# The end of a top-k decode put in another order: low parts of U made by VectorE, three transposes into one PSUM bank, one rounding by ScalarE, four stores on another queue

## The chip, the cores and the metric

One core of a Trainium2 chip runs the whole kernel. The metric is the device time of one execution in microseconds (us). Engines are named as in the profile: PE is TensorE, PEld its weight loads, DVE VectorE, ACT ScalarE, POOL GpSimd, SP SyncE, which only issues DMAs.

## What is computed

One encoder layer over 512 tokens: a projection, a spatial gating branch and an attention branch, and then a product-key expert layer (PEER). Only the last one touches the change:

```python
def block(xb):                                  # 128 tokens
    q = (xb @ w_query).reshape(PEER_TOKEN_BLOCK, PEER_HEADS, 2, D_KEY // 2)
    s = jnp.einsum('thpc,pkc->thpk', q, sub_keys)
    s1, i1 = lax.top_k(s[:, :, 0], PEER_TOPK)
    s2, i2 = lax.top_k(s[:, :, 1], PEER_TOPK)
    cand = (s1[..., :, None] + s2[..., None, :]).reshape(..., PEER_TOPK * PEER_TOPK)
    sc, ci = lax.top_k(cand, PEER_TOPK)
    e = (take_along_axis(i1, ci // PEER_TOPK) * N_KEYS + take_along_axis(i2, ci % PEER_TOPK))
    g = jax.nn.softmax(sc, axis=-1)
    act = jax.nn.gelu(jnp.einsum('td,thkd->thk', xb, expert_u[e]))
    return jnp.einsum('thk,thkd->td', g * act, expert_v[e])
```

There are 8 heads, 16 picks for each, 128 x 128 experts, width 1024.

## The kernel before

Three of the four token blocks (384 tokens) take the expert layer densely. For each of 128 slabs of 128 experts (here **unit** n, `prog["u"]`) TensorE multiplies the slab of U with the normed tokens. To keep float32 accuracy, U is cut into a high part and a low part: ScalarE casts `uraw` to `uhi` (`part`, L171), and `uraw - uhi` gives `ulo` (`part_lo`, L182). `product` (L202) then issues 24 matmuls of 128x384: 16 read `uhi`, the last 8 read `ulo`. `uraw`, `uhi`, `ulo` and the PSUM tiles `pu` have two buffers each, so `uhi` of unit n+2 may be written when the 16 of unit n are done, and the load of `uraw` n+2 when the low part of n is made. `flush` lets ScalarE read a finished unit through Gelu (`act`, L789) and so frees its bank. `ahead(n, limit)` issues the next n of these matmuls: it fills TensorE wherever other work is waited for, and 31 units (744 matmuls) are to be done by the end of the stretch described here.

The low part has two ways. While `prog["pool"]` is true, GpSimd makes it in two halves, the second half issued inside the product before. Once it is false, `los()` issues it whole on VectorE at the place where `los()` is called.

All engines run their instructions in program order. That order is written out by hand:

1. The loop over 16 query columns: query product, `scores`, two rounds of top 16 on VectorE (`top16`), candidates (`cand`, L648), `pick_head`. Every third head it appends a `decode`: a generator that turns positions into key indices and yields between its pieces. The pieces are: the position arithmetic on VectorE (L670 to L688), copies of `rw` and `cl` by ScalarE (L697, L698), comparisons and products on VectorE (L702 to L707), sums on VectorE (L711 to L717, which write `route`).
2. The decode's end: the pieces of heads 3 to 5 and then of heads 6 and 7, the softmax of the gates (`softmax`, L723 to L730) and stretches of `ahead` between.
3. `turn(0)`: `route` of the first block is transposed (L845), ScalarE writes the two index rows `idxT` and the gate `gT`, and VectorE rounds the gate (`gw`, L857) and takes the rest.
4. The pick loop, 48 slices of 8 tokens: VectorE makes one-hot rows `ohb` (L880) and weighted ones `oha` (L884), ScalarE the last two rows of `oha` (L895), TensorE multiplies them (L931, 16 small matmuls), ScalarE takes the result to `wst` (L911), which is stored to `wd`. Between the slices stand `ahead` calls that spread the rest of the 744 matmuls evenly, and `los()`.
5. After it the last four stores to `wd`, units 31 to 35 and then, to the end of the kernel, one loop in which unit products alternate with products with V (L1090).

Of the kernel before, what the change touches and what calls it, by code (L numbers as in the profile page):

```python
# [27 lines left out]
NK = 128  # L28
# [10 lines left out]
AHEAD = 31  # L39
GSCALE = 32768.0  # L40
# [6 lines left out]
def peer_block(ctx: ExitStack, tc: tile.TileContext, A, out):  # L47
    nc = tc.nc
    V, S, G, T, Q = nc.vector, nc.scalar, nc.gpsimd, nc.tensor, nc.sync
# [7 lines left out]
    pr = pr_ctx.enter_context(tc.tile_pool(name="pr", bufs=1, space=PSUM))  # L57
# [6 lines left out]
    wd = dram.tile([NWC, 128, NK, WTOK], F32, name="wd")  # L64
# [70 lines left out]
    ident = keep.tile([128, 128], F32, name="ident")  # L135
# [3 lines left out]
    iota_b = keep.tile([128, NK], BF16, name="iota_b")  # L139
# [37 lines left out]
    def part_lo(i, eng=G):  # L177

        if i in halves:
            hi, lo = parts[i]  # L180
            k = slice(4 * halves[i], 4 * halves[i] + 4 if eng is G else KT)
            eng.tensor_tensor(lo[:, k, :], raws[i][:, k, :], hi[:, k, :].bitcast(F32), op=ALU.subtract)  # L182
            halves[i] += k.stop // 4 - halves[i]
            if halves[i] == 2:
                del raws[i], halves[i]

    def los():
        for i in list(halves):
            part_lo(i, V)
# [116 lines left out]
    ps = []  # L306
# [30 lines left out]
    ps = []  # L337
# [5 lines left out]
    turning = heads_T("q", rot)  # L343
# [19 lines left out]
    ps = []  # L363
# [5 lines left out]
    turning = heads_T("k", rot)  # L369
# [14 lines left out]
    ps = []  # L384
# [10 lines left out]
    for b in range(NB):  # L395
        t = va[:, b, :]
# [76 lines left out]
    ps = []  # L473
# [91 lines left out]
    for b in range(NB):  # L565
        t = hs[b] = tk.tile([128, 1024], F32, name="xs", bufs=4)
# [45 lines left out]
    rt = rt_ctx.enter_context(tc.tile_pool(name="rt", bufs=1))  # L612
# [8 lines left out]
    def top16(lists):  # L621

        for m, ix, s in lists:
            V.max(m[:, 0:8], s)
        for m, ix, s in lists:
            V.max_index(ix[:, 0:8], m[:, 0:8], s)
        for m, ix, s in lists:
            V.match_replace(s, m[:, 0:8], s, NEG)
        for m, ix, s in lists:
            V.max(m[:, 8:16], s)  # L630
        for m, ix, s in lists:
            V.max_index(ix[:, 8:16], m[:, 8:16], s)
# [87 lines left out]
    def softmax(pool, top, g):  # L720

        PK = list(top.shape)
        V.tensor_tensor(g, top, top[:, :, :, 0:1].to_broadcast(PK), op=ALU.subtract)  # L723
        yield
        S.activation(g, g, AF.Exp)
        yield
        sm = pool.tile([128, 2, PK[1], PK[2]], F32, name="gsum")
        V.tensor_reduce(sm[:, 0], g, axis=AX.X, op=ALU.add)
        V.reciprocal(sm[:, 1], sm[:, 0])
        V.tensor_tensor(g, g, sm[:, 1, :, :, None].to_broadcast(PK), op=ALU.mult)  # L730
        yield
# [3 lines left out]
    route = [rt.tile([128, DB, H, TOPK], F32, name=f"route{i}") for i in range(3)]  # L735
# [30 lines left out]
    steps = []  # L766

    def step():
        while steps:
            if next(steps[0], True) is None:  # L770
                return
            steps.pop(0)

    def pick_head(h):
        cand = cands.pop(h)
        top16([(top[:, h, b, :], ci[:, h, b, :], cand[:, b, :]) for b in range(DB)])
        h0 = 0
        for n in HG:
            if h == h0 + n - 1:
                steps.append(decode(rt, iota_v, dense[1][:, h0:h0 + n], ci[:, h0:h0 + n], [r[:, h0:h0 + n] for r in by_head]))  # L780
            h0 += n
# [3 lines left out]
    def flush():  # L785
        if prog["gelu"] is not None:
            e, o = prog["gelu"]
            acts[e] = ring.tile([128, DT], F32, name="act")
            S.activation(acts[e], o[:, :DT], AF.Gelu_apprx_tanh)  # L789
            prog["gelu"] = None  # L790

    def ahead(n, limit):

        while n > 0:
            if prog["gen"] is None:
                if prog["u"] >= min(limit, NK):
                    return
                i = prog["u"] + NQ
                load(i + 2)
                part(i + 1)  # L800
                prog["gen"] = product(i, DT)
            o = next(prog["gen"])
            n -= 1
            if o is not None:
                flush()
                prog["gelu"] = (prog["u"], o)
                prog["gen"] = None
                prog["u"] += 1

    for c in range(NQ + 1):  # L810
# [4 lines left out]
        if c >= 1:  # L815
# [4 lines left out]
                cands[(c - 1) // 2] = candidates(rt, dense, (c - 1) // 2)  # L820
            elif c > 1:
                pick_head((c - 1) // 2 - 1)
    while steps:
        ahead(24, AHEAD)
        flush()
        step()
    pick_head(H - 1)
    gating = softmax(rt, top, by_head[2])
    next(gating)
    step()  # L830
    for _ in range(4):
        ahead(36, AHEAD)
        flush()
        next(gating, None)
        step()
    assert not steps or next(steps[0], True)
    tsc = {}

    def turn(b):

        rows = []
        for nm, t, dt, scale in (("i2T", route[1], BF16, 1.0), ("i1T", route[0], BF16, 1.0),
                                 ("gT", route[2], F32, GSCALE)):
            ps = pr.tile([128, 512], F32, name="po" if nm == "i2T" else "tr")
            T.transpose(ps[:, :128], t[:, b].rearrange("p h k -> p (h k)"), ident)  # L845
            if nm == "i2T":

                idx = rt.tile([128, 16, 2, 8, 2], BF16, name="idxT", bufs=2)
            r = idx[:, :, len(rows), :, :] if dt is BF16 else rt.tile([128, 16, 8, 2], F32, name=nm)
            S.activation(r, ps[:, :128].rearrange("p (g t) -> p g t", t=8)[:, :, :, None].to_broadcast([128, 16, 8, 2]),  # L850
                         AF.Copy, scale=scale)
            rows.append(r)
        gT = rows[2]
        yield

        gw = rt.tile([128, 16, 8, 2, 2], F16, name="gw", bufs=2)
        V.tensor_copy(gw[:, :, :, 0], gT)  # L857
        V.tensor_tensor(gw[:, :, :, 1], gT, gw[:, :, :, 0], op=ALU.subtract)

        gs = rt.tile([128, 16, 2], F32, name="gs", bufs=2)  # L860
        V.tensor_copy(gs[:, :, 0], gw[:, :, 7, 0, 0])
        V.tensor_tensor(gs[:, :, 1], gT[:, :, 7, 0], gs[:, :, 0], op=ALU.subtract)
        tsc[b] = (idx, gw, gs)
        yield

    drain(turn(0))
    prog["pool"] = False


    half = [128, 16, NK // 2, 2]  # L870

    def hots(t8):


        b, g = divmod(t8, 16)
        idx, gw, gs = tsc[b]
        pairs = lambda t: t.rearrange("p s t two -> p (s t) two")[:, :, None, :].to_broadcast(half)
        c = rt.tile([128, 16, NK], BF16, name="ohb", bufs=3)
        a = rt.tile([128, 16, NK], F16, name="oha", tag="oh", bufs=3)
        V.tensor_tensor(c.rearrange("p s (k two) -> p s k two", two=2),  # L880
                        iota_b.rearrange("p (k two) -> p k two", two=2)[:, None, :, :].to_broadcast(half),
                        pairs(idx[:, g]), op=ALU.is_equal)
        wide = [128, 7, 2, NK // 2, 2]
        V.tensor_tensor(a[:, 0:14].rearrange("p (t s) (k two) -> p t s k two", s=2, two=2),  # L884
                        c[:, 8:15, None].rearrange("p t o (k two) -> p t o k two", two=2).to_broadcast(wide),
                        gw[:, g, 0:7, :, None, :].to_broadcast(wide), op=ALU.mult)
        rest.append((a, c, gs, g))
        return a, c
# [9 lines left out]
    N8 = DT // 8  # L898
    per = WTOK // 8
    wst = None  # L900
    hot = [hots(0), hots(1)]
    gated()
    ahead(24, AHEAD)
    los()
# [8 lines left out]

    full = None

    def store(j):

        n = NK // per
        S.dma_start(wd[full[0], :, j * n:(j + 1) * n, :], full[1][:, j * n:(j + 1) * n, :])

    for t8 in range(N8):
        a, c = hot.pop(0)
# [3 lines left out]
        for q in range(2):  # L926
            pw = pr.tile([128, 4, NK], F32, name="acc", bufs=4)
            for j in range(4):
                for s in range(2):
                    t = 4 * q + j  # L930
# [7 lines left out]
        if t8 % 16 == 8 and t8 // 16 + 1 < DB:  # L938
            turning = turn(t8 // 16 + 1)
# [7 lines left out]
        if t8 % per == per - 1:  # L947
            full = (t8 // per, wst)
        if full is not None and t8 + 1 < N8:
            store((t8 + 1) % per)  # L950
    for j in range(per):
        store(j)
    ahead(10 ** 6, AHEAD)
    rt_ctx.close()
    pr_ctx.close()
# [204 lines left out]
    for e in range(NK):  # L1160
# [18 lines left out]
        n = min(int(quota), 128 - dotted)  # L1179
# [18 lines left out]
        if e == NK - 8:  # L1198
            assert issued == 128
            fg, *rest = [upool.tile([128, 1024], F32, name="fin", tag=t) for t in ("uraw", "uhi", "ulo") for _ in range(2)]  # L1200
            last = ex.tile([128, 2, 1024], F32, name="fin", tag="uv", bufs=UVB)
# [97 lines left out]
```

## Time and profile before

| | |
|---|---|
| median of 3 runs | 1474.46 us (1473.89 to 1474.46) |
| profiled execution | 1474.9 us, span 1473.1 us |
| PE busy | 1449.5 us (98%) |
| PEld busy | 1291.3 us (88%) |
| DVE busy | 1152.5 us (78%) |
| ACT busy | 658.0 us (45%) |
| POOL busy | 278.3 us (19%) |

The span runs from the first to the last instruction; the time of the execution has 1.8 us around it. Busy time of PE is modelled: its matmuls overlap, so the start of one and the start of the next say more than a length. In the rows below, what stands in brackets is the idle time of the engine before the row and who ended it.

### The profile page before, as it was taken

Reading aid. Unit: us, or ns where it says so; the run is one execution under the profiler, and the core shown is the slowest. Engines: PE = TensorE matmul, PEld = TensorE weight load, DVE = VectorE, ACT = ScalarE, POOL = GpSimd, SP = SyncE. Lnnn points to the kernel's source line nnn. Section 1 sums busy time; section 2 is a strip of 40 time slices with the busy share of each in tenths; the row PEclk is TensorE's granted clock in tenths of the full one; section 3 lists DMA queues with packets and bytes.
Section 4 is the critical chain, followed back from the end, with each engine's and each line's share of the span. In section 5 each row is a group of like instructions: output and inputs, shape, how many; then the busy total and the mean of one; then the engine's idle time right before and its main releaser. Section 6 shows DMA issues by size and latency. Waiting matters only on the chain.

```text
span 1473.1 us, 21706 instructions
## 1 busy us (share of the span) xinstructions
PE 1449.5 (98%) x7945; PEld 1291.3 (88%) x7945; DVE 1152.5 (78%) x2434; ACT 658.0 (45%) x1186; POOL 278.3 (19%) x222
## 2 busy tenths in 40 slices
PE   8999999999999999999999999999999999999997
PEld 6878988888999999999999999999999999988785
DVE  5745554999899949779888878888888888877865
ACT  4456743344578754433333333333333333333334
POOL 0140002445400000013131222222222222221000
PEclk9999999999999999999999999999999999999999
DMA  6331032232367776579999998999999999988764
GB/s 232 113 103 36 23 130 104 74 97 92 115 248 267 275 276 215 165 264 368 351 332 336 330 341 318 335 332 345 331 336 339 327 326 338 321 299 302 232 215 152
DMA packets 129067, 358.54 MB, mean 243 GB/s; under 512 B 9152, under 2 KB 59840, under 8 KB 112576
## 3 DMA queue, kind: packets, MB, share of 16 engines
q1 hardware_dynamic: 103328, 197.49, 40.5%
q0 software_dynamic: 18432, 134.23, 23.8%
q10 hardware_dynamic: 7200, 25.44, 4.3%
q8 instruction: 62, 1.02, 0.3%
q14 instruction: 45, 0.37, 0.1%
HBM read 327.10 MB, written 30.02 MB: 242 GB/s over the span
## 4 chain that ended last, share of the span: by engine, by line
PE 82%; DVE 11%; ACT 3%; issue 2%; DMA 1%; POOL 1%; ACTq 0%; SPq 0%; POOLq 0%; DVEq 0%
PE acc L1090 34%; PE pu L202 32%; PE acc L253 8%; DVE ohb L880 3%; DVE ulo L182 2%; DVE oha L884 2%; PE pu L253 1%; PE tr L440 1%; PE acc L453 1%; PE po L453 1%; DMA vraw<-in_uv_dram 1%; POOL ulo L182 1%; ACT uhi L171 1%; DMA uraw<-in_uT_dram 1%; PE pu L419 0%
## 5 line engine op out<-in xcount | busy, mean ns | idle before, releaser
L202 PE MATMUL pu<-h2T,uhi 128*128 128x384 f32 (+2 forms) x2336 | 450.2, 342 | 1.8 <-ACT uhi L171 0.9
L202 PEld LDWEIGHTS pu<-h2T,uhi 128*128 128x128 f32 x2336 | 408.8, 188 | 18.1 <-ACT uhi L171 1.2
L1025 POOL DMA_INDIRECT uv<-in_uv_dram,ei x128 | 172.1, 1344 | 664.4 <-DVE xlast L1040 295.9
L82 DVE TENSOR_TENSOR vlo<-vraw,vhi 128x1024 fp32r<-128x1024 f32 x126 | 154.4, 1226 | 152.6 <-ACT vhi L81 152.5
L81 ACT CAST vhi<-vraw 128x1024 fp32r<-128x1024 f32 x126 | 132.5, 1052 | 304.7 <-issue 193.3
L202 PE MATMUL pu<-h2T,ulo 128*128 128x384 f32 (+2 forms) x1168 | 235.1, 340 | 2.6 <-POOL ulo L182 2.6
L1090 PE MATMUL acc<-vhi,wahi 128*128 128x512 f32 x756 | 234.9, 391 | 0.0
L1090 PE MATMUL acc<-vlo,wahi 128*128 128x512 f32 x756 | 234.6, 391 | 0.0
L1090 PE MATMUL acc<-vhi,walo 128*128 128x512 f32 x756 | 234.2, 391 | 0.0
L202 PEld LDWEIGHTS pu<-h2T,ulo 128*128 128x128 f32 x1168 | 204.2, 188 | 7.8 <-POOL ulo L182 3.4
L1090 PEld LDWEIGHTS acc<-vlo,wahi 128*128 128x128 f32 x756 | 141.5, 188 | 32.4 <-DVE vlo L82 1.4
L1090 PEld LDWEIGHTS acc<-vhi,walo 128*128 128x128 f32 x756 | 141.5, 188 | 31.0 <-DVE walo L82 0.7
L171 ACT CAST uhi<-uraw 128x1024 fp32r<-128x1024 f32 x144 | 150.4, 1045 | 40.7 <-DMA uraw<-in_uT_dram 34.6
L1040 DVE SCALAR_TENSOR_TENSOR xlast<-uv,dot,xlast 128x1024 f32<-128x1024 f32 x128 | 164.4, 1285 | 4.5
L789 ACT ACTIVATE act<-pu 128x384 f32<-128x384 f32 x128 | 62.9, 491 | 232.9 <-PE pu L202 232.8
L1090 PEld LDWEIGHTS acc<-vhi,wahi 128*128 128x128 f32 x756 | 140.6, 188 | 23.5
L1031 DVE SCALAR_TENSOR_TENSOR uv<-uv,h 128x1024 f32<-128x1024 f32 x128 | 153.8, 1219 | 7.9 <-DMA uv<-in_uv_dram,ei 7.6
L182 DVE TENSOR_TENSOR ulo<-uraw,uhi 128x1024 fp32r<-128x1024 f32 x116 | 141.5, 1219 | 18.4 <-ACT uhi L171 12.1
L182 POOL TENSOR_TENSOR ulo<-uraw,uhi 128x512 fp32r<-128x512 f32 x56 | 79.3, 1439 | 198.3 <-PE acc L253 104.8
L1068 DVE TENSOR_TENSOR wa<-act,wt 128x384 f32<-128x384 f32 x128 | 70.5, 551 | 0.8 <-DMA wt<-wd 0.8
L82 DVE TENSOR_TENSOR walo<-wa,wahi 128x384 fp32r<-128x384 f32 x126 | 69.6, 552 | 0.6 <-ACT wahi L81 0.6
L81 ACT CAST wahi<-wa 128x384 fp32r<-128x384 f32 x126 | 64.1, 509 | 9.1 <-DVE wa L1068 9.1
(274 smaller groups left out, 1511.5 us busy)
## 6 DMA issues: line engine op xcount, KB each, us to landing
uraw<-in_uT_dram SPq DMA_DIRECT2D x128, 512.0 KB, 5.9
vraw<-in_uv_dram SPq DMA_DIRECT2D x128, 512.0 KB, 5.6
wd<-wst ACTq DMA_DIRECT2D x48, 512.0 KB, 3.6
wt<-wd SPq DMA_DIRECT2D x32, 768.0 KB, 11.1
wraw<-in_w_in_dram SPq DMA_DIRECT2D x19, 512.0 KB, 3.7
uraw<-in_w_q_dram SPq DMA_DIRECT2D x16, 512.0 KB, 3.9
xT<-in_xT_dram SPq DMA_DIRECT2D x8, 256.0 KB, 3.6
xt<-in_x_dram SPq DMA_DIRECT2D x1, 2048.0 KB, 11.1
```

The costliest lines, as they stand in the source:

```text
L81: S.copy(hi, src)
L82: sub.tensor_tensor(lo, src, hi.bitcast(F32), op=ALU.subtract)
L171: S.copy(hi, raws[i])
L182: eng.tensor_tensor(lo[:, k, :], raws[i][:, k, :], hi[:, k, :].bitcast(F32), op=ALU.subtract)
L202: T.matmul(o, l[:, k, :], r[:, k, t0:n], start=(p == 0 and k == 0), stop=(p == 2 and k == KT - 1))
L253: T.matmul(out[b], l[:, b * 128:(b + 1) * 128], r[:, kk, :], start=(k == 0 and i == 0), stop=(k == KT - 1 and i == 2))
L789: S.activation(acts[e], o[:, :DT], AF.Gelu_apprx_tanh)
L1025: G.indirect_dma_start(out=uvs[r].rearrange("p s d -> p (s d)"), out_offset=None, in_=A["uv"], in_offset=bass.IndirectOffsetOnAxis(ap=ei[: ...
L1031: V.scalar_tensor_tensor(uv[:, 0, :], uv[:, 0, :], 1.0, h2, op0=ALU.mult, op1=ALU.mult, accum_out=d[:, 0:1])
L1040: V.scalar_tensor_tensor(xlast, uv[:, 1, :], d[:, 1:2], xlast, op0=ALU.mult, op1=ALU.add)
L1068: eng.tensor_tensor(wa.rearrange("p (c t) -> p c t", c=NWC), acts.pop(e).rearrange("p (c t) -> p c t", c=NWC), wts[e // WG][:, :, e % WG, ...
L1090: T.matmul(acc[b][n], l[:, c], r[:, n * 512:(n + 1) * 512], start=(e == 0 and i == 0), stop=(e == NK - 1 and i == 2))
```

## The change

Four edits, all between the end of the query columns and the last stores to `wd`:

- `prog["pool"] = False` moves from behind `turn(0)` to the end of the query columns. From there on VectorE makes the low parts; `chunk(n)` is `ahead(n)`, `los()`, `flush()`.
- The pieces of the two decodes and of the softmax are issued in another order, with 204 matmuls between them instead of 240 (12 more are issued at the end of the query columns in both). So `turn(0)` comes after 216 unit matmuls instead of 252, and the first slice after 240 instead of 276; the pick loop's `ahead` calls share the other 504 instead of 468.
- `turn` puts its three transposes into one bank. ScalarE reads it four times: two index rows, `gT`, and the gate rounded to 16 bits (`gw`), which VectorE did before. The first `ohb` is issued ahead of the rest of `turn(0)` (`match`).
- The last four stores to `wd` are issued by SP instead of ACT.

```diff
-    while steps:
-        ahead(24, AHEAD)
+
+    prog["pool"] = False
+
+    def chunk(n):
+        ahead(n, AHEAD)
+        los()
         flush()
-        step()
+
+    chunk(24)
+    step()
     pick_head(H - 1)
+    last = steps.pop()
     gating = softmax(rt, top, by_head[2])
     next(gating)
+    chunk(24)
     step()
-    for _ in range(4):
-        ahead(36, AHEAD)
-        flush()
-        next(gating, None)
-        step()
-    assert not steps or next(steps[0], True)
+    next(last)
+    chunk(24)
+    step()
+    step()
+    next(gating)
+    next(last)
+    next(last)
+    chunk(36)
+    next(gating)
+    next(last)
+    chunk(36)
+    next(last)
+    chunk(36)
+    chunk(24)
+    assert not steps and next(last, True) and next(gating, True)
...
     def turn(b):
...
+        ps = pr.tile([128, 512], F32, name=("tr", "po")[b % 2])
+        for j, t in enumerate((route[1], route[0], route[2])):
+            T.transpose(ps[:, j * 128:(j + 1) * 128], t[:, b].rearrange("p h k -> p (h k)"), ident)
...
-        V.tensor_copy(gw[:, :, :, 0], gT)
+        for j, r, scale in ((0, idx[:, :, 0], 1.0), (1, idx[:, :, 1], 1.0), (2, gT, GSCALE), (2, gw[:, :, :, 0], GSCALE)):
+            src = ps[:, j * 128:(j + 1) * 128].rearrange("p (g t) -> p g t", t=8)
+            S.activation(r, src[:, :, :, None].to_broadcast([128, 16, 8, 2]), AF.Copy, scale=scale)
+        yield idx
         V.tensor_tensor(gw[:, :, :, 1], gT, gw[:, :, :, 0], op=ALU.subtract)
...
-    drain(turn(0))
-    prog["pool"] = False
...
-    hot = [hots(0), hots(1)]
+    turning = turn(0)
+    first = match(next(turning)[:, 0])
+    drain(turning, 1)
+    hot = [hots(0, first), hots(1)]
...
-    def store(j):
+    def store(j, eng=S):
...
     for j in range(per):
-        store(j)
+        store(j, Q)
```

Three places show how instructions move. The first is VectorE's queue behind the candidates of the last head (`cand`). Before:

```order
L648 TENSOR_TENSOR cand<-s_2179 128x3x8
L702 TENSOR_TENSOR oh<-oh,iota_v 128x1728 x2
L705 TENSOR_TENSOR oh<-oh,fi 128x9x64
L707 TENSOR_TENSOR oh<-oh,fi 128x9x128
```

With the change:

```order
L648 TENSOR_TENSOR cand<-s_2179 128x3x8
L182 TENSOR_TENSOR ulo<-uraw,uhi 128x1024
L624 MAX top<-cand 128x8 x3
L626 MAX_INDEX ci<-top,cand 128x8 x3
L628 MATCH_REPLACE cand<-top,cand 128x54 x3
L630 MAX top<-cand 128x8 x3
L632 MAX_INDEX ci<-top,cand 128x8 x3
L723 TENSOR_TENSOR route_2188<-top 128x8x3x16
L182 TENSOR_TENSOR ulo<-uraw,uhi 128x1024
L702 TENSOR_TENSOR oh<-oh,iota_v 128x1728 x2
```

The low parts of units 2 and 3 now stand in this queue, the first behind all the work of the query columns; the last head's top 16 stands ahead of the comparisons of heads 3 to 5.

The second place is ScalarE's queue around the table load for the softmax (L725) and the copies of the second decode (`oh<-rw`, `oh<-cl`). Before:

```order
L725 ACT_TABLE_LOAD
L725 ACTIVATE route_2188<-route_2188 128x8x3x16
L171 CAST uhi<-uraw 128x1024 x2
L789 ACT_TABLE_LOAD
L789 ACTIVATE act<-pu 128x384
L697 CAST oh<-rw 128x6x128
L698 CAST oh<-rw 128x6x64
L697 CAST oh<-cl 128x6x128
L698 CAST oh<-cl 128x6x64
L171 CAST uhi<-uraw 128x1024
L789 ACTIVATE act<-pu 128x384 x2
```

With the change:

```order
L789 ACTIVATE act<-pu 128x384
L725 ACT_TABLE_LOAD
L725 ACTIVATE route_2188<-route_2188 128x8x3x16
L697 CAST oh<-rw 128x6x128
L698 CAST oh<-rw 128x6x64
L697 CAST oh<-cl 128x6x128
L698 CAST oh<-cl 128x6x64
L171 CAST uhi<-uraw 128x1024
L789 ACT_TABLE_LOAD
L789 ACTIVATE act<-pu 128x384 x2
L171 CAST uhi<-uraw 128x1024 x2
```

The cast of unit 5 and the Gelus of units 3 and 4 (with the table load they need) now stand behind the copies, which wait for VectorE's `rw` and `cl`. Before, two casts and a Gelu stood ahead of them.

The third place is ScalarE's queue at the first two slices, with the change:

```order
L868 ACTIVATE idxT<-tr 128x16x16 x2
L868 ACTIVATE gT<-tr 128x256
L868 ACTIVATE gw<-tr 128x128x2
L907 ACTIVATE oha<-ohb,gs 128x128 x4
L171 CAST uhi<-uraw 128x1024
L789 ACTIVATE act<-pu 128x384
L171 CAST uhi<-uraw 128x1024
```

The cast behind the four `oha` rows is that of unit 10, whose first matmul follows the first slice on TensorE. Before, the cast at this place was that of a unit that began later, since the first slice stood in the middle of unit 11.

## Rows read from the trace of the kernel before

**Rows 1.** The page: the span, and the first row of its first part (busy us, share of the span, instructions).

```profile
span 1473.1 us, 21706 instructions
...
PE 1449.5 (98%) x7945; PEld 1291.3 (88%) x7945; DVE 1152.5 (78%) x2434; ACT 658.0 (45%) x1186; POOL 278.3 (19%) x222
```

**Rows 2.** Busy time by stretch, in us from the span's start: from TensorE's wait for its first late work to the middle of the decode, the pick loop, the units behind it, and the long loop. Columns: length, then busy time (and instructions) of PE, PEld, DVE, ACT and POOL, the granted TensorE clock as a share of full speed, DMA share, GB/s.

```profile
351.46:375.00 23.54, 20.20 (x105) 19.05 (x105) 23.40 (x125) 9.69 (x14) 17.09 (x9) 0.93 0.26 90
...
395.37:527.82 132.45, 129.97 (x1243) 121.28 (x1242) 129.20 (x122) 105.30 (x236) 0.00 (x0) 1.00 0.67 248
527.82:541.53 13.71, 12.84 (x76) 12.52 (x74) 3.67 (x3) 4.92 (x8) 0.47 (x2) 1.00 0.94 345
541.53:1310.00 768.47, 768.47 (x3896) 700.80 (x3896) 633.37 (x1098) 289.45 (x501) 162.18 (x119) 1.00 0.89 316
```

**Rows 3.** TensorE in order of time: start, length, engine, line, operation, out<-in, count. The first is the last third of unit 2, the next two those of unit 5 and the start of unit 6; 379.31 and 383.47 begin units 8 and 9.

```profile
351.46 1.55 PE L202 MATMUL pu<-h2T,ulo 128*128 128x384 f32 x8
...
367.69 2.89 PE L202 MATMUL pu<-h2T,ulo 128*128 128x384 f32 x8 [2.56 <-POOL ulo L182]
370.38 3.55 PE L202 MATMUL pu<-h2T,uhi 128*128 128x384 f32 x16
...
379.31 2.93 PE L202 MATMUL pu<-h2T,uhi 128*128 128x384 f32 x16
...
383.47 2.93 PE L202 MATMUL pu<-h2T,uhi 128*128 128x384 f32 x16
...
395.37 0.33 PE L931 MATMUL acc<-oha,ohb 128*128 128x128 f16 x3
```

**Rows 4.** VectorE in order of time through the two decodes, with one row of GpSimd (POOL) that lies beside it.

```profile
343.46 0.47 DVE L670 CAST cf<-ci 128x144 f16<-128x144 uint32 x1
...
345.81 2.55 POOL L182 TENSOR_TENSOR ulo<-uraw,uhi 128x512 fp32r<-128x512 f32 x2 [1.96 <-ACT uhi L171]
345.88 2.56 DVE L680 TENSOR_TENSOR at<-at,mk 128x144 f16<-128x144 f16 x2
...
349.26 0.59 DVE L648 TENSOR_TENSOR cand<-s 128x48 f32<-128x48 f32 x5
...
359.65 2.02 DVE L702 TENSOR_TENSOR oh<-oh,iota_v 128x1728 bf16<-128x1728 bf16 x2
...
363.66 0.82 DVE L711 TENSOR_TENSOR oh<-oh 128x576 bf16<-128x576 bf16 x2
...
366.41 0.45 DVE L624 MAX8 top<-cand 128x8 f32<-128x54 f32 x3
...
368.77 0.55 DVE L723 TENSOR_TENSOR route<-top 128x384 f32<-128x384 f32 x1
369.23 1.30 DVE L670 CAST cf<-ci 128x96 f16<-128x96 uint32 x1
...
373.27 0.45 DVE L680 TENSOR_TENSOR at<-at,mk 128x96 f16<-128x96 f16 x2
...
376.67 0.54 DVE L728 TENSOR_REDUCE gsum<-route 128x24 f32<-128x384 f32 x1
...
377.58 0.74 DVE L730 TENSOR_TENSOR route<-route,gsum 128x384 f32<-128x384 f32 x1
```

**Rows 5.** ScalarE in order of time: the table load for Gelu, the first of the second decode's four copies, and the cast behind them.

```profile
376.45 1.28 ACT L789 ACT_TABLE_LOAD   x1
...
378.14 0.82 ACT L697 CAST oh<-rw 128x768 bf16<-128x768 int32 x1
...
380.42 1.05 ACT L171 CAST uhi<-uraw 128x1024 fp32r<-128x1024 f32 x1
```

**Rows 6.** One microsecond of the stretch after TensorE's wait at 367.69, with the columns of rows 2.

```profile
369.00:370.00 1.00, 1.00 (x3) 1.00 (x4) 1.00 (x2) 0.00 (x0) 1.00 (x1) 0.50 0.18 33
```

**Rows 7.** The start of the pick loop: VectorE's rest of the gate and its first two one-hot rows, and ScalarE's cast behind the four `oha` rows.

```profile
392.34 0.42 DVE L858 TENSOR_TENSOR gw<-gT,gw 128x256 f16<-128x256 f32 x1
...
392.98 1.21 DVE L880 TENSOR_TENSOR ohb<-iota_b,idxT 128x2048 bf16<-128x2048 bf16 x1
...
395.24 1.22 DVE L880 TENSOR_TENSOR ohb<-iota_b,idxT 128x2048 bf16<-128x2048 bf16 x1
...
397.09 1.04 ACT L171 CAST uhi<-uraw 128x1024 fp32r<-128x1024 f32 x1
```

**Rows 8.** Late in the pick loop: two slices on TensorE with 10 unit matmuls between them, and VectorE's one-hot rows with a low part between.

```profile
518.80 1.07 PE L931 MATMUL acc<-oha,ohb 128*128 128x128 f16 x16
...
521.51 1.07 PE L931 MATMUL acc<-oha,ohb 128*128 128x128 f16 x16
...
518.89 1.22 DVE L880 TENSOR_TENSOR ohb<-iota_b,idxT 128x2048 bf16<-128x2048 bf16 x1
...
523.41 1.22 DVE L182 TENSOR_TENSOR ulo<-uraw,uhi 128x1024 fp32r<-128x1024 f32 x1
524.54 1.22 DVE L880 TENSOR_TENSOR ohb<-iota_b,idxT 128x2048 bf16<-128x2048 bf16 x1
```

**Rows 9.** Behind the pick loop: ACT issues the last four stores (ACTq is its queue of DMA issues), casts unit 32, and TensorE begins it.

```profile
528.84 3.12 ACTq L919 DMA_DIRECT2D wd<-wst  x4
532.00 1.04 ACT L171 CAST uhi<-uraw 128x1024 fp32r<-128x1024 f32 x1 [3.19 <-issue]
...
533.10 3.05 PE L202 MATMUL pu<-h2T,uhi 128*128 128x384 f32 x16 [0.87 <-ACT uhi L171]
```

More of the change, by code (lines that the diff above doesn't have):

```diff
@@ L837, in peer_block @@
+    chunk(24)
[12 more added lines that the diff above has]
+    assert not steps and next(last, True) and next(gating, True)
     tsc = {}
     def turn(b):
[L841 to L852, printed above, removed]
@@ L853, in turn @@
-        gT = rows[2]
-        yield
+        ps = pr.tile([128, 512], F32, name=("tr", "po")[b % 2])
+        for j, t in enumerate((route[1], route[0], route[2])):
+            T.transpose(ps[:, j * 128:(j + 1) * 128], t[:, b].rearrange("p h k -> p (h k)"), ident)
+        idx = rt.tile([128, 16, 2, 8, 2], BF16, name="idxT", bufs=2)
+        gT = rt.tile([128, 16, 8, 2], F32, name="gT")
         gw = rt.tile([128, 16, 8, 2, 2], F16, name="gw", bufs=2)
-        V.tensor_copy(gw[:, :, :, 0], gT)
+        for j, r, scale in ((0, idx[:, :, 0], 1.0), (1, idx[:, :, 1], 1.0), (2, gT, GSCALE), (2, gw[:, :, :, 0], GSCALE)):
+            src = ps[:, j * 128:(j + 1) * 128].rearrange("p (g t) -> p g t", t=8)
+            S.activation(r, src[:, :, :, None].to_broadcast([128, 16, 8, 2]), AF.Copy, scale=scale)
@@ L864, in turn, with match, hots @@
         yield
-    drain(turn(0))
-    prog["pool"] = False
     half = [128, 16, NK // 2, 2]
-    def hots(t8):
+    def match(ix):
+        c = rt.tile([128, 16, NK], BF16, name="ohb", bufs=3)
+        V.tensor_tensor(c.rearrange("p s (k two) -> p s k two", two=2),
+                        iota_b.rearrange("p (k two) -> p k two", two=2)[:, None, :, :].to_broadcast(half),
+                        ix.rearrange("p s t two -> p (s t) two")[:, :, None, :].to_broadcast(half), op=ALU.is_equal)
+        return c
+    def hots(t8, c=None):
         b, g = divmod(t8, 16)
         idx, gw, gs = tsc[b]
-        pairs = lambda t: t.rearrange("p s t two -> p (s t) two")[:, :, None, :].to_broadcast(half)
-        c = rt.tile([128, 16, NK], BF16, name="ohb", bufs=3)
+        c = match(idx[:, g]) if c is None else c
         a = rt.tile([128, 16, NK], F16, name="oha", tag="oh", bufs=3)
-        V.tensor_tensor(c.rearrange("p s (k two) -> p s k two", two=2),
-                        iota_b.rearrange("p (k two) -> p k two", two=2)[:, None, :, :].to_broadcast(half),
-                        pairs(idx[:, g]), op=ALU.is_equal)
         wide = [128, 7, 2, NK // 2, 2]
@@ L914, in peer_block @@
     full = None
-    def store(j):
+    def store(j, eng=S):
         n = NK // per
-        S.dma_start(wd[full[0], :, j * n:(j + 1) * n, :], full[1][:, j * n:(j + 1) * n, :])
+        eng.dma_start(wd[full[0], :, j * n:(j + 1) * n, :], full[1][:, j * n:(j + 1) * n, :])
     for t8 in range(N8):
```

## The prediction, as it was written before the result was known

> **What bounds the kernel now.** I read the page first: TensorE is busy 98% of the span [rows 1]. By stretch, it is busy without a gap from 541.53 us on, through the long loop [rows 2]. The order of work there is unchanged, so whatever the change does to the moment at which TensorE begins unit 34 (541.53) moves the end by the same amount, and the whole question lies between 339 and 541 us. I then read TensorE in order of time. A unit costs 4.16 us (379.31 to 383.47) [rows 3], so 0.173 us for each matmul; a slice with 10 unit matmuls costs 2.71 us (518.80 to 521.51) [rows 8]. By these prices the pick loop's 48 slices with 468 matmuls need 48 x 2.71 - 12 x 0.17 = 128 us, and about 1 us for six transposes; rows 2 show 132.45 us to the end of unit 30, so about 3.7 us are lost. VectorE sets that: two slices and a low part take it 5.65 us (518.89 to 524.54), of which the low part is 1.13, so 2.26 for a slice [rows 8]; 48 slices, 20 low parts and twice the rounding of the gates make 134 us, and it is busy 129.20 of 132.45 [rows 2]. Ahead of the loop TensorE loses about 5 us, mostly at 365 to 372: 2.56 us of waiting for GpSimd's low part, and then slow matmuls (16 in 3.55 us instead of 2.93) [rows 3] at a granted clock of 0.50, the lower level of 1.2 GHz [rows 6]. Behind the loop it loses 0.87 us on a cast that stood behind four stores, whose issue kept ScalarE's queue for 3.12 us [rows 9].
>
> **Low parts by VectorE: the first wait.** The low part of unit 2 now stands behind the last `cand` on VectorE. That ended at 359.65 [rows 4]. It comes 2.1 us earlier now: at 345.88 two small sums took 2.56 us while GpSimd's pair ran beside them, and the same two take 0.45 without it [rows 4], and this pair of halves is gone. So the low part runs from 357.6 to 358.8. TensorE wants it at 351.46 [rows 3]. It waits 7.3 us where before it waited 0.7 (for a Gelu). What is queued behind on TensorE is only more units; what it does next depends on VectorE again.
>
> **The second wait.** Behind that low part (1.14 to the next start), VectorE runs the top 16 of the last head (366.41 to 368.77, 2.36), the subtraction (to 369.23, 0.46), the low part of unit 3 (1.14), comparisons and products of heads 3 to 5 (359.65 to 363.66, 4.01), the position arithmetic of heads 6 and 7, and the low part of unit 4 (1.22) [rows 4]. The arithmetic took 7.44 us (369.23 to 376.67) beside GpSimd; the nine-list form took 5.80 (343.46 to 349.26), 3.7 without the 2.1 above. For six lists I take 3.5, an estimate from these. The sum is 357.6 + 1.14 + 2.36 + 0.46 + 1.14 + 4.01 + 3.5 + 1.22 = 371.4 for the low part of unit 4. TensorE has finished units 2 and 3 and two thirds of unit 4 by 367 to 369, even with some microseconds at the lower clock. It waits again, until 371.4, and ends unit 4 at 372.8.
>
> **The third wait.** Unit 5 needs the bank of unit 3, so the Gelu of unit 3. That Gelu now stands behind the second decode's four copies, the cast of unit 5 and a table load. The copies wait for VectorE's `rw`, at about 369.85; they take 2.28 us (378.14 to 380.42), the cast 1.05, table load and Gelu 1.69 (376.45 to 378.14) [rows 5]: 375.0. TensorE idles 2.2 us more.
>
> **To the first slice.** Units 5 to 8 take 4 x 4.16, to 391.6. VectorE is ahead by then: 371.4 + 2.75 (sums, 363.66 to 366.41) + 1.14 + about 1.6 for the softmax (376.67 to the end of 377.58 + 0.74) + 2.7 and 1.9 (two thirds of the nine lists' 4.01 and 2.75) + 2.3 for two low parts = 383.8 for the routes [rows 4]. So the transposes wait for TensorE's own units, not for the decode. Transposes and unit 9 take 0.4 + 4.16: the first slice starts at 396.1, against 395.37 before [rows 3], and with 36 matmuls fewer behind it (6.2 us).
>
> **One bank, one rounding.** ScalarE's four readings follow each other; before, the third transpose waited for a bank, and rounding took VectorE until 392.34. The first `ohb` starts 0.9 us after the transposes' end, and the remaining 0.64 (392.34 to 392.98) [rows 7] comes behind it. This is worth 1 to 1.5 us of VectorE at each of three blocks, but TensorE is the later of the two here, so I cost it at nothing at the start; its cover is unit 9 (4.16 us).
>
> **The first cast of the loop.** Unit 10 follows the first slice at once. Its cast stands behind four `oha` rows, the last two of which need the second `ohb`; before, the cast began 1.85 us after that `ohb` did (395.24 to 397.09) and took 1.04 [rows 7]. With `ohb` at 392.9, 0.64 for the gate and 2.26 for the first slice, the second starts at 395.8, the cast ends at 398.7, and TensorE is there at 397.0: a wait of 1.7.
>
> **The loop.** 48 slices and 504 matmuls cost TensorE 48 x 2.71 + 24 x 0.17 + 1.0 = 135.2. VectorE needs 48 x 2.26 + 21 x 1.14 + 1.9 = 134.3, from 392.9, and so ends some 3 us before TensorE: the bound changes from VectorE to TensorE, and of the 3.7 us lost before I take 0.3.
>
> **The stores.** ScalarE is rid of 3.12 us of issue; TensorE's 0.87 [rows 9] goes, so -0.9. The cover is that units 31 and 32 (8.3 us) lie between the stores and the unit whose load is now behind them on SP.
>
> **The sum.** 396.1 + 135.2 + 1.7 + 0.3 = 533.3 for the end of unit 30, and 0.9 for the lower clock after the waits at 369 and 373: 534.2 against 527.82 [rows 2], so +6.4; with the stores' -0.9, +5.5 us. The profiled execution was 1474.9 us, so 1480.4 by its own time; the median of the runs shown is 0.44 lower: 1479.9 us.
>
> **Bounds.** The clock costs 0 to 2.0: the 8 and 16 matmuls from 367.69 took 2.89 and 3.55 us instead of 1.55 and 2.93 [rows 3], part of it a wait for the second half. I take 0.9, about the middle, since these waits are as long as that one, but the slow time may fall into the third of them. The loop's loss is 0 to 3.7. The wait for the cast is 0 to 1.7: the upper end, since ScalarE's queue leaves no other order. The stores give 0 to 1.2. With all ends on one side +2.3 and +10.9: 1476.8 to 1485.4 for this course alone.
>
> **The rivals.** *Freed VectorE, faster.* GpSimd's low parts hold VectorE up: 2.1 us at 345.88, 3.9 in the second decode's arithmetic [rows 4], and more in its sums. Taking them off VectorE's way is the gain, if TensorE keeps its old pace: it was through unit 8 at 383.47 [rows 3], VectorE has the routes at 383.8, the first slice starts at 388.6, the loop ends at 388.6 + 137.2 = 525.8, and with the stores the kernel takes 1471.6. It decides from the point where TensorE ends unit 8 before 386; three waits of together some 12 us speak against it. The Trainium skill, SBUF — State Buffer, "Who interferes with whom", says that a VectorE instruction with two SBUF inputs and a GpSimd one that reads SBUF exclude each other for the whole instruction. The trace agrees with it (2.56 against 0.45 us), and by that rule alone the change gains what this rival says. Chance 0.12.
>
> *The waits overlap, no change.* If the Gelu of unit 3 is in time, unit 5 starts at 372.8, the first slice at 393.9; with no loss to the clock or the cast the loop ends at 529.1, +1.3, and the stores take it to +0.4: 1474.9. Against it stands ScalarE's order. Chance 0.18.
>
> *SP's queue, slower still.* The load of unit 33 now follows four stores of 0.5 MB, about 6 us at the 345 GB/s of that stretch [rows 2], on one queue. If it lands later than 7.3 us after unit 30, TensorE waits, up to about 3 us: 1483. Chance 0.1.
>
> **Chances.** My course has 0.6. About 0.2% (3 us) is what a measurement can tell from no change here. My course ends under +3 us in 0.06 of all cases, so: slower 0.64, same 0.24, faster 0.12. The range for 8 in 10 takes in the case without change and SP's case: 1473.5 to 1485.
>
> **What would show it.** TensorE waiting for VectorE's `ulo` for about 7 us near 351, again near 369, and for a Gelu near 373; GpSimd idle from 344 on; the small sums at 0.45 or less; the first slice near 396 with 240 matmuls done; PE and not DVE without gaps in the pick loop; no wait for a cast near 535. Wrong would be: VectorE's `cand` done long before 357 (then the first wait shrinks), the lower clock lasting through units 5 to 8 (+8 and more), or slices that still come late in the loop.

## The result, and the profile after

The changed kernel takes 1485.42 us in the median of 6 runs (1483.84 to 1486.48), the kernel before 1474.46 us (1473.55 to 1475.14): a ratio of 1.007, with a 95% interval of 1.0059 to 1.0081. It is slower by 11 us. The profiled execution took 1486.09 us. Its page, against [rows 1]:

```profile
span 1484.3 us, 21694 instructions
...
PE 1450.9 (98%) x7945; PEld 1294.1 (87%) x7945; DVE 1152.1 (78%) x2441; ACT 658.4 (44%) x1189; POOL 248.0 (17%) x202
```

TensorE's busy time, which is modelled, grew by 1.4 us only; the other 10 are gaps. TensorE in order of time, from unit 2 to the first slice, as [rows 3] show it for before (columns as there):

```profile
358.18 2.93 PE L202 MATMUL pu<-h2T,ulo 128*128 128x384 f32 x8 [7.23 <-DVE ulo L182]
360.90 3.70 PE L202 MATMUL pu<-h2T,uhi 128*128 128x384 f32 x16
...
370.39 1.68 PE L202 MATMUL pu<-h2T,ulo 128*128 128x384 f32 x8 [1.62 <-DVE ulo L182]
376.85 5.49 PE L202 MATMUL pu<-h2T,uhi 128*128 128x384 f32 x16 [4.77 <-ACT act L789]
382.14 1.96 PE L202 MATMUL pu<-h2T,ulo 128*128 128x384 f32 x8
383.94 2.93 PE L202 MATMUL pu<-h2T,uhi 128*128 128x384 f32 x16
...
396.43 0.49 PE L860 MATMUL tr<-ident,route 128*128 128x128 f32 x3
...
400.92 1.07 PE L946 MATMUL acc<-oha,ohb 128*128 128x128 f16 x16
```

The three waits that were forecast stand there, in their order: 7.23 us for the low part of unit 2, 1.62 for that of unit 4, and 4.77 for the Gelu of unit 3, ahead of unit 5. Behind the third, 24 matmuls (376.85 to 383.94) take 7.1 us instead of 4.16. What ScalarE did ahead of that Gelu, and VectorE ahead of the two low parts:

```profile
368.95 0.83 ACT L697 CAST oh<-rw 128x768 bf16<-128x768 int32 x1 [2.91 <-DVE rw L685]
...
372.81 0.83 ACT L697 CAST oh<-cl 128x768 bf16<-128x768 int32 x1 [2.61 <-DVE route L717]
...
373.96 1.04 ACT L171 CAST uhi<-uraw 128x1024 fp32r<-128x1024 f32 x1
375.01 1.28 ACT L789 ACT_TABLE_LOAD   x1
376.31 0.87 ACT L789 ACTIVATE act<-pu 128x384 f32<-128x384 f32 x2
...
345.20 0.50 DVE L680 TENSOR_TENSOR at<-at,mk 128x144 f16<-128x144 f16 x2
...
356.91 1.22 DVE L182 TENSOR_TENSOR ulo<-uraw,uhi 128x1024 fp32r<-128x1024 f32 x1
...
369.12 1.22 DVE L182 TENSOR_TENSOR ulo<-uraw,uhi 128x1024 fp32r<-128x1024 f32 x1
...
372.37 0.73 DVE L717 TENSOR_TENSOR route<-oh 128x144 f32<-128x144 bf16 x2
```

The second pair of copies (`oh<-cl`) stands 2.61 us still until VectorE's L717 has read the last sums of heads 3 to 5. One-hot tiles `oh` have three buffers; heads 3 to 5 hold two until that L717 and the first new tile takes the third. Behind the pair wait a cast, a table load and the Gelu.

By stretch (columns as in [rows 2]): two microseconds inside unit 5, the pick loop, and the six units behind it.

```profile
378.00:380.00 2.00, 2.00 (x8) 2.00 (x7) 2.00 (x6) 0.11 (x1) 0.00 (x0) 0.50 0.44 178
...
400.92:537.29 136.37, 134.95 (x1279) 127.62 (x1279) 130.81 (x122) 108.33 (x241) 0.00 (x0) 1.00 0.67 252
537.29:564.52 27.23, 25.56 (x146) 24.92 (x145) 8.53 (x9) 9.97 (x14) 0.47 (x2) 1.00 0.70 242
```

And what answers to [rows 9]: SP (SPq) now issues the stores, with loads of `uraw` behind them; ScalarE's casts for units 33 and 36 wait for those loads, and TensorE for the casts.

```profile
536.19 2.85 SPq L934 DMA_DIRECT2D wd<-wst x4
539.14 2.40 SPq L164 DMA_DIRECT2D uraw<-in_uT_dram  x2
...
545.32 1.05 ACT L171 CAST uhi<-uraw 128x1024 fp32r<-128x1024 f32 x1 [3.18 <-DMA uraw<-in_uT_dram]
...
546.42 3.07 PE L202 MATMUL pu<-h2T,uhi 128*128 128x384 f32 x16 [0.64 <-ACT uhi L171]
...
559.13 1.04 ACT L171 CAST uhi<-uraw 128x1024 fp32r<-128x1024 f32 x1 [3.57 <-DMA uraw<-in_uT_dram]
...
560.23 3.06 PE L202 MATMUL pu<-h2T,uhi 128*128 128x384 f32 x16 [1.03 <-ACT uhi L171]
```

**Where the 11.2 us of span lie.** This execution came to the change 0.68 us earlier (unit 0 begins at 338.70; before at 339.38). From there to the first slice it took 62.2 us against 56.0 (+6.2, with 36 matmuls fewer in it); in the loop 136.37 against 132.45 (+3.9, with the 36 in it); for units 31 to 36 27.23 against 26.2 (+1.0); and +0.7 in all that follows.

### The profile page after: what moved, and what is told of

Its sections match the earlier page's. It is cut to its first block, busy times and chain, and to the rows that moved or that the text cites. A ratio compares the mean times of both kernels' runs of the same rounds, so it can differ in the third digit from the quotient of the medians.

```text
span 1484.3 us, 21694 instructions
## 1 busy us (share of the span) xinstructions
PE 1450.9 (98%) x7945; PEld 1294.1 (87%) x7945; DVE 1152.1 (78%) x2441; ACT 658.4 (44%) x1189; POOL 248.0 (17%) x202
## 4 chain that ended last, share of the span: by engine, by line
PE 86%; DVE 6%; DMA 5%; ACT 2%; issue 1%; SPq 0%; ACTq 0%; DVEq 0%
PE pu L202 38%; PE acc L1105 31%; PE acc L253 6%; PE acc L946 3%; DMA vraw<-in_uv_dram 3%; PE pu L253 1%; DMA uraw<-in_uT_dram 1%; PE tr L440 1%; DMA wraw<-in_w_in_dram 1%; PE acc L453 1%; PE po L453 1%; PE tr L755 1%; DVE vlo L82 1%; PE pu L419 0%; PE pu L418 0%
## 5 line engine op out<-in xcount | busy, mean ns | idle before, releaser
L182 DVE TENSOR_TENSOR ulo<-uraw,uhi 128x1024 fp32r<-128x1024 f32 x126 | 153.8, 1221 | 33.2 <-ACT uhi L171 32.8
L182 POOL TENSOR_TENSOR ulo<-uraw,uhi 128x512 fp32r<-128x512 f32 x36 | 48.7, 1375 | 180.5 <-PE acc L253 104.6
```

## The experiments

Each was timed in five rounds, and each ratio stands against runs of the kernel before on the same chip, whose medians were 1474.6 to 1475.3. e1, e2, e5, e6 and e7 alter one thing in the changed kernel, e3 and e4 do one part alone in the kernel before, and the others put parts together.

**e1, the last stores back on ScalarE's queue.**

```
-        store(j, Q)
+        store(j)
```

> The changed kernel with the last four stores back on ScalarE's queue. Theory (the stores on SP's queue hold up the loads behind them): the casts of units 33 and 36 come in time, TensorE's waits of 0.64 and 1.03 us for them go, a wait of some 0.9 us before unit 32 comes back, and the time falls by 0.5 to 2 us, to 1483.4 to 1484.9. Rival (the stores are harmless on SP, everything lies before the pick loop's end): the wait before unit 32 comes back and the time is the same or 0.9 us longer, 1485.4 to 1486.3.

Measured: 1483.01 us, ratio 1.0052 (1.0039 to 1.0065), 2.4 us less than the changed kernel and 0.4 under the range expected. The two intervals just overlap, but each of the 5 runs lies below each of the changed kernel's 6.

```profile
537.73 2.89 ACTq L934 DMA_DIRECT2D wd<-wst  x4
540.66 1.05 ACT L171 CAST uhi<-uraw 128x1024 fp32r<-128x1024 f32 x1 [2.44 <-issue]
...
541.77 3.05 PE L202 MATMUL pu<-h2T,uhi 128*128 128x384 f32 x16
```

The stores still hold ScalarE for 2.44 us, but unit 32 comes right behind unit 31, against both expectations, and neither 33 nor 36 waits: units 31 to 36 take 25.38 us instead of 27.23. Moving the stores to SP saved nothing in the new order and cost about 2 us of waits for loads.

**e2, all low parts by GpSimd again until the first transposes.** `prog["pool"] = False` stands behind the turn of the first picks again, and in `chunk`:

```
-        los()
+        if not prog["pool"]:
+            los()
```

> The changed kernel with GpSimd making the low parts until the first transposes, as before; the new order, the one bank and the stores stay. Theory (low parts behind VectorE's backlog are the larger cause): the wait of 7.2 us at unit 2 goes, GpSimd and VectorE hold each other up again, and with the copies' wait left the time is 1477 to 1481. Rival (the new order of the decode's pieces is the cause, above all the copies that wait for VectorE): TensorE still stands before unit 5 and the time stays at 1483 or above.

Measured: 1483.8 us, ratio 1.0065 (1.0052 to 1.0078). No wait for a low part is left, and one wait took their place:

```profile
361.50 0.52 ACT L725 ACTIVATE route<-route 128x384 f32<-128x384 f32 x1 [7.09 <-DVE route L723]
368.33 0.83 ACT L697 CAST oh<-rw 128x768 bf16<-128x768 int32 x1 [6.31 <-DVE rw L685]
...
371.04 0.83 ACT L697 CAST oh<-cl 128x768 bf16<-128x768 int32 x1 [1.47 <-DVE route L717]
...
375.08 5.48 PE L202 MATMUL pu<-h2T,uhi 128*128 128x384 f32 x16 [14.41 <-ACT act L789]
```

Unit 5 starts only 1.8 us earlier. Its Gelu stands in ScalarE's queue behind an exponential and copies that wait for VectorE's decode, whoever makes the low parts. The new order costs 9 us with the low parts on GpSimd, as before; 2.4 of that are the stores on SP (e1), so some 6.5 are the order of the decode, with the earlier turn in it.

**e3, one bank with the gate rounded by ScalarE, alone.** In `turn` of the kernel before, the three tiles and readings replaced by those of the new `turn`, without the early `ohb`.

> The kernel before with only the turn of the picks changed: all picks of a group go into one bank and the gate is rounded by ScalarE. Everything else, the order of the decode and GpSimd's low parts included, as before. Theory (this part is worth nothing or a little, as it was costed): 1472.5 to 1475 us, that is 0 to -2 against 1474.5. Rival (this part carries some of the 11 us that the change lost): 1477 us or more, and a new wait for ACT at the turns in the pick loop.

Measured: 1474.41 us, ratio 1.0001 (0.9992 to 1.001). By itself, in the old order, this part is worth nothing that can be measured.

**e4, low parts by VectorE alone.** In the kernel before: `prog["pool"] = False` ahead of the decode's end, and `los()` behind each stretch of units, in the old order.

> The kernel before with one edit: VectorE makes the low parts from the end of the query columns on; the old order, the old transposes and the old stores stay. Theory (the low part of unit 2 behind VectorE's backlog is a loss that the old order cannot take back): TensorE waits some 7 us at unit 2, then runs without waits, reaches the transposes about 3.7 us later than before, and the time is 1477 to 1480. Rival (freeing VectorE from GpSimd gains more than it costs, and only the new order loses): 1474 or less.

Measured: 1480.98 us, ratio 1.0054 (1.0032 to 1.0076), 1 us above what was expected. One of the 12 runs, of 1500.64 us, lifts the ratio; the medians give 1.004, 6 us.

```profile
359.36 2.93 PE L202 MATMUL pu<-h2T,ulo 128*128 128x384 f32 x8 [7.23 <-DVE ulo L182]
...
396.35 0.33 PE L848 MATMUL po<-ident,route 128*128 128x128 f32 x1 [1.89 <-DVE route L717]
...
404.54 1.07 PE L933 MATMUL acc<-oha,ohb 128*128 128x128 f16 x16
```

The last 8 us of that, with the columns of [rows 2]:

```profile
396.35:404.54 8.19, 7.55 (x28) 7.15 (x28) 5.47 (x9) 3.43 (x9) 0.00 (x0) 0.58 0.05 19
```

The first wait is the same 7.23 us. The 2.56 us that TensorE waited at unit 5 are gone for it, but VectorE, with the low parts among its pieces, has the routes later: the transposes wait 1.89 us, and the matmuls behind them run at a mean clock of 0.58. Counted from unit 0, the transposes come 6.1 us later than before (3.7 expected) and the first slice some 9. The pick loop gives 1.9 of that back (130.57 us from there to the end of unit 30).

**e5, a buffer of its own for the tile that waited.** In the decode of two heads, the second one-hot tile from memory that isn't in use yet (that of `wst`):

```
+            if pool is rt and nh == 2 and r is cl:
+                oh = pool.tile([128, n, TOPK + K8, K8], BF16, name="ohl", tag="wst", bufs=2)
```

> The changed kernel with a buffer of its own for the last one-hot tile of the second decode (in the space of the tile that the pick loop fills later), so that its copy doesn't wait for a buffer of the first decode. Theory (the copies' wait of 2.6 us for that buffer, which holds the Gelu of unit 3 and so unit 5, is on the path): unit 5 starts some 2.4 us earlier and the time is 1481 to 1483.3, the lower end if the time at the lower clock gets shorter too. Rival (the table load and the cast set unit 5's start anyway): 1484.5 to 1486.

Measured: 1482.83 us, ratio 1.0055 (1.004 to 1.007), 2.6 us less. The interval overlaps the changed kernel's, and the 6 runs spread from 1480.63 to 1488.61; the trace is clearer.

```profile
375.23 4.97 PE L202 MATMUL pu<-h2T,uhi 128*128 128x384 f32 x16 [1.75 <-ACT act L792]
```

The second pair of copies (`ohl<-cl`) no longer stands behind L717. Counted from unit 0, unit 5 starts 2.7 us earlier and the first slice comes 3.6 earlier. The wait that the forecast lacked, for the buffer, is worth about 2.6 us.

**e6, only unit 2's low part back to GpSimd.** As e2, with `prog["pool"] = False` behind the first stretch.

> The changed kernel, but GpSimd still makes the low part of unit 2, so that the 7.2 us wait at its last third is gone. Theory (unit 5's start is set by ScalarE's queue, so that the first wait only comes earlier than the one that would stand there anyway): unit 5 starts within 1.5 us of where it did, the wait for act grows from 4.8 to 10 us or more, and the time is 1483 to 1486. Rival (the first wait counts in full, as the prediction had it): 1477 to 1480.

Measured: 1487.84 us, ratio 1.0087 (1.0073 to 1.0101), above both ranges.

```profile
346.68 1.32 DVE L685 TENSOR_SCALAR rw<-ai 128x144 int32<-128x144 int32 x1
...
363.99 2.93 PE L202 MATMUL pu<-h2T,ulo 128*128 128x384 f32 x8 [7.54 <-DVE ulo L182]
...
378.71 5.49 PE L202 MATMUL pu<-h2T,uhi 128*128 128x384 f32 x16 [4.79 <-ACT act L789]
```

This did not do what it was made for: the wait did not vanish but moved to unit 3, whose low part now had the same place in VectorE's queue. Unit 5 starts where it did (0.5 us later, counted from unit 0), and the wait for `act` did not grow. It shows that the first wait belongs to a place in VectorE's order, not to a unit. The two theories were not told apart by it; e2, where no low part holds TensorE and unit 5 still starts only 1.8 us earlier, and e10 bear on that. Nor does it show why the median is 2.4 us above the changed kernel's: in the profiled execution, the longest of the five, only 0.4 us of the difference stand ahead of the first slice, 1.5 in units 31 to 36 and the rest ahead of unit 0 and behind unit 36.

**e7, the last decode's copies one step later.** Only the order of the pieces in the list is altered, so that the cast of unit 5 and the Gelu of unit 3 enter ScalarE's queue ahead of the copies:

```
     next(gating)
     next(last)
-    next(last)
     chunk(36)
+    next(last)
     next(gating)
-    next(last)
     chunk(36)
     next(last)
     chunk(36)
+    next(last)
     chunk(24)
```

> The changed kernel with one number altered: the last decode's copies on ScalarE come a step later in the stream of matmuls, so that the cast of unit 5 and the Gelu of unit 3 stand ahead of them in ScalarE's queue. Theory (the copies, which wait for a one-hot buffer, hold up that Gelu and so unit 5): the 4.8 us wait for act is gone or under 1 us, unit 5 starts near 372, and the time is 1478 to 1481. Rival (something else holds unit 5, or what is won there is lost again at the turn of the routes): 1484 or more.

Measured: 1479.16 us, ratio 1.0027 (1.0018 to 1.0036), 6.3 us less than the changed kernel.

```profile
368.27 0.49 ACT L789 ACTIVATE act<-pu 128x384 f32<-128x384 f32 x1
...
370.50 1.66 PE L202 MATMUL pu<-h2T,ulo 128*128 128x384 f32 x8 [1.14 <-DVE ulo L182]
372.00 2.93 PE L202 MATMUL pu<-h2T,uhi 128*128 128x384 f32 x16
```

Unit 5 follows unit 4 without a wait, at the full clock. Against the changed kernel the first slice comes 7.8 us earlier (393.14): 4.8 of the wait and 2.9 of the slow matmuls behind it. Of that, 6.3 are seen in the medians; in the profiled execution 1.8 are lost again behind unit 36.

**e9, both mended.** e7's order and e1's store together.

> The changed kernel with two things mended at once: the last decode's copies a step later, as in e7, and the last stores from ScalarE's queue, as in e1. Theory (the two costs lie in different places and add): 1479.2 less 2.4 is 1476 to 1478 us, no wait for act at unit 5, no waits for uhi after unit 30. Rival (they overlap): 1479 or more.

Measured: 1476.97 us, ratio 1.0015 (1.0006 to 1.0025). The two add: 1479.16 less 2.2. The 7.23 us wait at unit 2 is still in it, and a second for unit 4's low part:

```profile
371.54 1.97 PE L202 MATMUL pu<-h2T,ulo 128*128 128x384 f32 x8 [2.15 <-DVE ulo L182]
373.31 4.25 PE L202 MATMUL pu<-h2T,uhi 128*128 128x384 f32 x16
```

Up to the end of the pick loop the order is that of e7, where the same wait was 1.14 us and the 16 matmuls of unit 5 took 2.93. VectorE starts the low part of unit 4 30.4 us behind unit 0 in both; TensorE came to it later in e7, since its 16 matmuls behind the first wait had taken 4.18 us against 3.17 here. So the first slice lies 55.91 us behind unit 0 here and 54.33 in e7: 1.6 us that no edit made.

**e10, e9 without the first wait.** GpSimd makes the low parts of units 2 to 4.

> As e9, and GpSimd makes the low parts until the last decode begins (units 2 to 4), so that the 7.2 us wait at unit 2 has nothing to stand on, now that the copies no longer hold unit 5. Theory (with the later wait mended the first one counts, but the softmax on ScalarE still has to be done before the Gelu of unit 3): no wait for low parts over 1 us, a wait for act of some 6 us at unit 5, which starts between 366 and 369 instead of 372, and 1471 to 1474.5 us. Rival (unit 5 is held until 371 or later by VectorE's decode, made slower by GpSimd's work): 1475.5 or more. If the first wait counted in full: 1469 to 1470.

Measured: 1475.97 us, ratio 1.001 (1.0001 to 1.0019), above the range of its theory and only 1 us less than e9, which the intervals do not part; in the two profiled executions the first slice is 3.2 us earlier than in e9, counted from unit 0, and 1.6 earlier than in e7.

```profile
362.77 0.53 ACT L725 ACTIVATE route<-route 128x384 f32<-128x384 f32 x1 [6.38 <-DVE route L723]
...
366.08 5.49 PE L202 MATMUL pu<-h2T,uhi 128*128 128x384 f32 x16 [3.65 <-ACT act L789]
373.80 1.66 PE L202 MATMUL pu<-h2T,ulo 128*128 128x384 f32 x8 [2.23 <-DVE ulo L182]
```

Of 9.4 us of waiting in e9, 5.9 come back, and with them slow matmuls (16 in 5.49 us). VectorE is what TensorE waits for, through ScalarE's exponential and then through the low part of unit 5: it is busy 26.72 us of the 27 from 345 to 372 in this kernel, as in the changed one (26.76) and the one before (26.86).

**e8, put together.** GpSimd makes the low parts of units up to 4, VectorE from unit 5 on, between the pieces of the last decode; the Gelus stand ahead of the softmax; the routes are turned after 240 matmuls; one bank and the early `ohb` as in the change; the second slice's one-hot rows stand behind the 24 matmuls that follow the turn, so that the cast of unit 10 no longer waits for them; stores on ScalarE. The heart of it, behind two stretches of 24 in the old order:

```
    ahead(24, AHEAD)
    prog["pool"] = False
    ahead(16, AHEAD)
    low()            # los(); flush()
    step()
    step()
    ahead(24, AHEAD)
    low()
    pick_head(H - 1)
```

> A version put together from what the runs so far showed: GpSimd makes the low parts of units up to 4, VectorE those from unit 5 on; VectorE's low parts stand between the pieces of the last decode; the routes are turned after 240 matmuls; one bank with the gate by ScalarE; the stores from ScalarE's queue as before. Theory (the change's parts are sound where no wait stands in TensorE's order): no wait over 1.5 us on TensorE between 345 and 400, first slice of the pick loop near 389 to 392, 1467 to 1471 us. Rival (a new wait takes it back): 1473 or more.

Measured: 1468.48 us, ratio 0.9957 (0.9943 to 0.9971): 6 us faster than the kernel before, 17 faster than the changed one. The waits of TensorE from 330 to 600 us (in total, times, longest), all of them:

```profile
PE pu L202 <- ACT act L789: 0.7, 1, 0.7
PE acc L956 <- DVE oha L904: 0.6, 2, 0.4
PE tr L868 <- DVE route L717: 0.5, 1, 0.5
```

Four of the decode's last sums on VectorE, and the first slice:

```profile
383.25 1.12 DVE L714 TENSOR_TENSOR oh<-oh 128x384 bf16<-128x384 bf16 x4
...
389.52 1.07 PE L956 MATMUL acc<-oha,ohb 128*128 128x128 f16 x16
```

And the stretch up to 372, where TensorE, too, is busy nearly all the time, at the full clock:

```profile
345.00:372.00 27.00, 26.28 (x151) 25.83 (x151) 26.90 (x141) 14.43 (x18) 7.57 (x6) 1.00 0.36 119
```

**e11, e8 with all low parts by GpSimd until the turn.**

> The put-together version e8, but GpSimd makes all low parts until the routes are turned, as in the kernel before, so that only VectorE's low parts from unit 5 on are taken back. Theory (those low parts on VectorE are what frees the end of the decode from the shared slowness with GpSimd): a wait for POOL or for route comes back, first slice 3 to 6 us later than e8's 389.5, 1471 to 1475 us. Rival (e8's gain comes from the earlier turn and the new order alone): 1467.5 to 1469.5.

Measured: 1474.22 us, ratio 0.9999 (0.999 to 1.0008).

```profile
386.70 3.24 DVE L714 TENSOR_TENSOR oh<-oh 128x384 bf16<-128x384 bf16 x4
...
390.56 0.85 PE L868 MATMUL tr<-ident,route 128*128 128x128 f32 x3 [3.06 <-DVE route L717]
```

The same four sums that took 1.12 us in e8 take 3.24 beside GpSimd. So 6 us of e8 come from VectorE's low parts from unit 5 on, and none that can be measured from the rest of it alone.

## Why the prediction was right on the direction and 5.5 us too low

Forecast were 1479.9 us and slower with a chance of 0.64; it became 1485.42, slower, 0.4 us above the upper end of the range. That it lies at the upper end of the course's own bounds (1485.4) is chance: they put up to 3.7 us in the loop, where nothing was lost beyond the cast, and had no term for the buffer. By its steps, with the 0.68 us that this execution was ahead added to the measured times:

- **The first wait** was sized right: the low part of unit 2 from 357.6 to 358.8, and 7.23 us of waiting (7.3 said). The pair of small sums took 0.50 (0.45 said, from the row of the smaller pair, of six lists).
- **The second wait** came as said, for the low part of unit 4: 371.0 against 371.4. The arithmetic of heads 6 and 7 took 3.1 us (366.00 to 369.12) where 3.5 was taken from the nine-list form.
- **The third wait is the step that failed in size.** Unit 5 was put at 375.0 and started at 377.5. `rw` was in time (369.6 against 369.85); the second pair of copies was costed as running behind the first, and it stood for a buffer that heads 3 to 5 give back with their last sums. In the kernel before, those sums lay far ahead of the copies, so no row of before shows this wait; the three buffers of `oh` do, in the code. e5 gives its price, about 2.6 us, and e7 the whole third wait with what follows it, 6.3.
- **The clock** was taken at 0.9 us, with 2.0 as its upper bound, from a wait of 2.56 us that lies in the same rows as the slow matmuls [rows 3, 6]. Behind the third wait it was 2.9: 24 matmuls in 7.1 us, at a granted clock of 0.50 (378 to 380 us). That is 2.0 more than the sum had, and the bound was too low as well. The first wait had its own slow matmuls (2.93 and 3.70 us), which the second wait covered, as was reasoned.
- **Units 6 to 8, transposes, unit 9**: 17.0 us from 383.94 to 400.92, as said. The first slice came at 401.6 against 397.0 with the forecast's clock in it; the buffer and the clock are those 4.6 us.
- **One bank and the loop**: right. e3 shows nothing, the loop took 136.37 us against 137.2, of which 1.4 for the cast of unit 10 (1.7 said) and no other loss. TensorE is the bound, busy 134.95, and VectorE 130.81.
- **The stores had the wrong sign**: forecast -0.9 us, measured +1.0. This is the rival of SP's queue, in a smaller size than its 3 us: units 33 and 36 wait 0.64 and 1.03 us, since loads stand behind 2 MB of stores. The cover of two units that the sum named was too short by 0.64 us for the first of these loads, and it named nothing for unit 36. And the 0.87 us that the move was to save was gone by the new order itself (e1).

So 4.6 us were missing up to the first slice and 1.9 behind the loop, and 0.8 too many stood in the loop: 5.7 of span, of which 5.5 are seen in the medians.

The rivals: *freed VectorE, faster* fell for this order, but e8 and e11 show that its mechanism is real: with the low parts on VectorE only where TensorE doesn't want them at once, it is worth 6 us. The Trainium skill (SBUF — State Buffer, "Who interferes with whom") says that VectorE's instructions with two SBUF inputs, or in a two-port mode, and GpSimd's that read SBUF shut each other out. The four sums, which have two inputs each, agree: 3.24 us in e11 against 1.12 in e8. L685, with one input, took 1.32 us in e6 beside GpSimd against 0.23 in the changed kernel; whether in a two-port mode, no row shows. *The waits overlap, no change* fell because ScalarE's order held; e7, where it is altered, ends 4.6 us above before, because the first wait, the second and the stores stay.

The parts do not add: the low parts alone cost 6 us (e4), the order of the decode some 6.5 (e2), one bank nothing (e3), the stores 2.4 (e1): 15 by addition, and 11 together. A wait early in TensorE's stream is paid only as far as no later one would have stood there; e2 and e10, where the first wait goes and a later one comes or grows, show it from the other side.

What stays open: e10 won 3.2 us in the trace and 1 in the median. The profiled executions of e9 and e10 lie at the opposite ends of their runs (1478.14 of 1475.98 to 1478.14, and 1474.68 of 1474.68 to 1478.74), and half of the 3.2 is the 1.6 us by which e9's execution differs from e7's in the same order: where TensorE stayed slow longer behind the first wait (e7), the second one was shorter, and the matmuls behind it were not slow. What decides that, and what moves the rest of the spread of some 2 us from one execution to the next, no run shows.

## What to carry to other kernels

When a step is moved in an in-order queue, go through what each of its instructions needs to begin, free buffers too, and not only its data: a ring of buffers that was never full in the old order may be full in the new one, and the trace of before can't show it. Price a late instruction by what stands behind it on its engine, and price a wait on TensorE together with the slow matmuls that follow it. Taking work off GpSimd, beside which VectorE was slower here, is worth something only where VectorE, which takes it over, isn't the late one at that moment.

## What the runs showed of the hardware that was not expected

The price of the lower clock did not grow with the wait ahead of it: 16 matmuls of one unit took 5.49 us behind a wait of 4.77 us (changed kernel), 5.48 behind one of 14.41 (e2) and 5.49 behind one of 3.65 (e10), against 2.93 at full clock. Nor was it the same behind the same wait: behind the first one, of 7.23 or 7.24 us, the 24 matmuls that followed took 6.3 us in the changed kernel, 5.7 in e4 and 6.8 in e7, against 4.16. In e7 unit 5, which followed a wait of 1.14 us for the end of unit 4, lost nothing; in e9, where that wait was 2.15, its 16 matmuls took 4.25 us.
